# Low weight parts made during the feed-forward and fetched later from DRAM; a branch's input split in halves

## Chip, core and metric

The kernel runs on one core of a Trainium2 chip. It is one program with one instruction stream for each engine: TensorE (PE in the profile; its weight loads are PEld), VectorE (DVE), ScalarE (ACT), GpSimd (POOL) and SyncE (SP), whose stream here only issues DMAs. The metric is the device time in microseconds (us) of one execution, the median of several runs.

## What is computed

Two transformer blocks in a row on 512 tokens of width 1024. The first is a recurrent mixer, a gated feed-forward and a small gate. The second has two attentions and a feed-forward with 16384 experts. What the change touches, from the reference:

```python
def hybrid_layer(...):            # first block
    ...                           # mixer; x = x + merged @ w_out
    h = rmsnorm(x, g_ffn)
    g, u = jnp.split(h @ w_gate_up, 2, axis=-1)
    x = x + (jax.nn.silu(g) * u) @ w_down          # the feed-forward
    gate = jax.nn.sigmoid(rmsnorm(x, g_ple) @ w_ple_gate)
    x = x + gate * (p_i @ w_ple)

def compress(t, w1, w2):          # second block, keys (kv = 0) and values (kv = 1)
    blk = t[:, cmp_idx] + cmp_pos[:, None, :]
    blk = blk.transpose(0, 1, 3, 2, 4).reshape(B, n_cmp, G, CMP_LEN * dk)
    return jax.nn.gelu(blk @ w1) @ w2

def peer_ffn(x, w_q, sub_keys, expert_u, expert_v):
    q = _rms((xt @ w_q).reshape(T, P_HEADS, P_KEY_DIM)).astype(x.dtype)   # queries
    s1 = jnp.einsum('thd,hnd->thn', q[..., :half], sub_keys[:, 0])
    s2 = jnp.einsum('thd,hnd->thn', q[..., half:], sub_keys[:, 1])
    v1, i1 = lax.top_k(s1, P_TOPK)
    v2, i2 = lax.top_k(s2, P_TOPK)
    ...                           # 16 experts e and weights g for each token and head
    a = jnp.einsum('cd,ckd->ck', xc, expert_u[ec])
    w = (gc * jax.nn.gelu(a)).astype(x.dtype)
    return jnp.einsum('ck,ckd->cd', w, expert_v[ec])
```

## The kernel before

**Products.** A float32 product is made of three products of a narrower type (F32R). Each operand is split into a high part (ACT casts it, L58) and a low part (the operand less its high part, on DVE or POOL, L59). `mm3` (L71 to L73) then adds high x high, high x low of the activations and low x high of the weights in PSUM. Weights come in tiles of 128 x 1024. `weights` loads one over SP into `wraw` (three buffers) and splits it into `whi` and `wlo` (two buffers each). `linear` does that and runs 24 matmuls of 512 columns on it.

**Stages**, in the times of the profiled execution. The mixer of the first block lasts to about 369 us. The feed-forward runs from there to some 750 us: 44 `linear`s on `w_gu`, then 8 sums over three pieces of `w_down`. `ple` follows with 8 `linear`s on `w_ple_gate`. The second block's attentions begin near 800 us with the two compressed branches. Its output product ends near 1134 us. The queries of the expert part run to about 1354 us, a table of one-hot products (`build`) to 1532 us, and the dense product over all experts to the end.

**Compressed branches** (`compress`, keys first, then values). From the projection a tile `blk` is made, 128 x 16 x 64. ACT and DVE (for the values POOL) split it into `bs`, of which there is one buffer. Four tiles of `w1` follow, each with 8 matmuls (L949, L950).

**Queries** (`queries`). For each of 8 heads two tiles of `peer_w_q` are multiplied. The low part of the first is made on DVE, of the second on POOL. Between the heads DVE picks the 16 best keys of each half (`choose_steps`), and once, beside heads 0 and 1, it scales the input by its norm (`normalise`: xn, then xsh on ACT and xsl on DVE). All products from head 2 on need that scaled input. Beside the heads run the first chunks of the dense expert part. `hidden` takes one chunk of 128 experts of U (`peer_ut`), multiplies it (24 matmuls of 384 columns into psA) and applies the gelu. The first 16 calls make the chunks of `AWAY` (35, 41, ..., 125), whose results are spilled to DRAM; then come chunks 0, 1, 2 and so on. Nine calls stand between the heads and eleven behind them.

**Order.** The program is written with the Tile language. Its scheduler lays the instructions of each engine into one fixed order, by a simulated time, and each engine then runs its list strictly in that order. A DMA of SP that waits for a buffer holds up all of SP's later DMAs.

## Time and profile before

| | us |
|---|---|
| median of 3 runs (2426.09 to 2430.34) | 2426.5 |
| the profiled execution, its own time | 2424.03 |
| span of its instructions | 2422.3 |
| PE busy, of that span | 2365.4 |
| feed-forward, 369 to 631 us: PE busy | 262.0 of 262 |
| compressed branches, 840 to 865 us: PE busy | 18.0 of 25 |
| queries, 1134 to 1354 us: PE busy | 200.5 of 220 |

PE is busy in 98% of the span, so the table is read for where it is not. Two places stand out: the compressed branches and the first 70 us of the queries. A row of a timeline gives start and duration, engine, line, operation, output and inputs, and in brackets the idle time before it and whose result ended that. A row of the waits gives the total, how often, and the longest. In a row by stages every engine has its busy time, and PEclk is the clock granted to PE as a share of full speed.

### The profile page before, as it was taken

Reading aid. Unit: us, or ns where it says so; the run is one execution under the profiler, and the core shown is the slowest. Engines: PE = TensorE matmul, PEld = TensorE weight load, DVE = VectorE, ACT = ScalarE, POOL = GpSimd, SP = SyncE. Lnnn points to the kernel's source line nnn. Section 1 sums busy time; section 2 is a strip of 40 time slices with the busy share of each in tenths; the row PEclk is TensorE's granted clock in tenths of the full one; section 3 lists DMA queues with packets and bytes.
Section 4 is the critical chain, followed back from the end, with each engine's and each line's share of the span. In section 5 each row is a group of like instructions: output and inputs, shape, how many; then the busy total and the mean of one; then the engine's idle time right before and its main releaser. Section 6 shows DMA issues by size and latency. Waiting matters only on the chain.

```text
span 2422.3 us, 34482 instructions
## 1 busy us (share of the span) xinstructions
PE 2365.4 (98%) x12831; PEld 2027.7 (84%) x12831; DVE 1779.3 (73%) x3426; ACT 1018.3 (42%) x1634; POOL 688.1 (28%) x693
## 2 busy tenths in 40 slices
PE   8999999999999999999799999999899999999999
PEld 7888888888888777677688999998798889989887
DVE  7777664555435658776899898796788878889797
ACT  5444343222224466763344555433333333333333
POOL 1000001000011204334455000255555555555441
PEclk9999999999999999999899999999999999999999
DMA  4232322222333331002133555648999999999895
GB/s 134 96 105 90 102 96 96 96 96 96 97 96 108 106 105 44 1 1 84 59 119 128 179 218 207 226 160 290 333 332 348 350 341 326 351 347 360 302 342 203
DMA packets 166072, 434.37 MB, mean 179 GB/s; under 512 B 15120, under 2 KB 71312, under 8 KB 164368
## 3 DMA queue, kind: packets, MB, share of 16 engines
q1 hardware_dynamic: 126736, 294.80, 36.1%
q0 software_dynamic: 36864, 134.23, 14.8%
q10 hardware_dynamic: 2304, 3.15, 0.3%
q8 instruction: 100, 1.64, 0.3%
q14 instruction: 68, 0.56, 0.1%
HBM read 401.71 MB, written 30.41 MB: 178 GB/s over the span
## 4 chain that ended last, share of the span: by engine, by line
PE 44%; DVE 5%; DMA 2%; ACT 1%; issue 1%; POOL 0%; ACTq 0%; DVEq 0%; POOLq 0%
PE ps L1792 7%; PE ps L1793 7%; PE psA L73 7%; PE psA L71 7%; PE ps L1791 7%; PE psA L72 6%; PE ps L1733 3%; DMA wraw<-peer_ut 1%; DVE wlo L59 1%; DMA wraw<-peer_v 1%; PE ps L73 0%; PE ps L71 0%; DVE ix L1583 0%; PE ps L72 0%; DVE ix L1580 0%
## 5 line engine op out<-in xcount | busy, mean ns | idle before, releaser
L58 ACT CAST whi<-wraw 128x1024 fp32r<-128x1024 f32 (+3 forms) x322 | 330.3, 1026 | 708.9 <-issue 250.1
L59 DVE TENSOR_TENSOR wlo<-wraw,whi 128x1024 fp32r<-128x1024 f32 (+2 forms) x314 | 387.6, 1235 | 205.4 <-ACT whi L58 197.3
L71 PE MATMUL psA<-xsh,whi 128*128 128x384 f32 x1024 | 346.6, 339 | 3.6 <-ACT whi L58 3.3
L73 PE MATMUL psA<-xsh,wlo 128*128 128x384 f32 x1024 | 345.3, 337 | 4.0 <-DVE wlo L59 4.0
L72 PE MATMUL psA<-xsl,whi 128*128 128x384 f32 x1024 | 343.5, 335 | 0.0
L72 PE MATMUL ps<-xl,whi 128*128 128x512 f32 x864 | 337.3, 390 | 4.3 <-DVE xl L64 4.3
L73 PE MATMUL ps<-xh,wlo 128*128 128x512 f32 x864 | 337.8, 391 | 0.5 <-DVE wlo L59 0.5
L71 PE MATMUL ps<-xh,whi 128*128 128x512 f32 x864 | 336.8, 391 | 0.7 <-ACT whi L58 0.5
L1792 PE MATMUL ps<-vl,wh 128*128 128x512 f32 x768 | 299.9, 390 | 3.9 <-DVE vl L59 3.9
L1793 PE MATMUL ps<-vh,wl 128*128 128x512 f32 x768 | 298.1, 389 | 0.0
L1791 PE MATMUL ps<-vh,wh 128*128 128x512 f32 x768 | 243.8, 390 | 4.5 <-ACT vh L58 4.5
L304 POOL TENSOR_TENSOR sq<-sq,sqt 128x512 f32<-128x512 f32 x18 | 28.8, 1601 | 711.9 <-ACT sqt L303 708.3
L71 PEld LDWEIGHTS psA<-xsh,whi 128*128 128x128 f32 x1024 | 192.4, 188 | 10.6 <-ACT whi L58 4.5
L73 PEld LDWEIGHTS psA<-xsh,wlo 128*128 128x128 f32 x1024 | 192.2, 188 | 8.2 <-DVE wlo L59 5.6
L72 PEld LDWEIGHTS ps<-xl,whi 128*128 128x128 f32 x864 | 162.5, 188 | 39.5 <-DVE xl L64 5.5
L72 PEld LDWEIGHTS psA<-xsl,whi 128*128 128x128 f32 x1024 | 192.4, 188 | 2.9
L73 PEld LDWEIGHTS ps<-xh,wlo 128*128 128x128 f32 x864 | 162.4, 188 | 36.9 <-DVE wlo L59 3.2
L71 PEld LDWEIGHTS ps<-xh,whi 128*128 128x128 f32 x864 | 162.5, 188 | 35.2 <-ACT whi L58 1.0
L58 ACT CAST wh<-w 128x384 fp32r<-128x384 f32 x128 | 65.7, 513 | 255.0 <-issue 150.5
L1792 PEld LDWEIGHTS ps<-vl,wh 128*128 128x128 f32 x768 | 144.1, 188 | 32.2 <-DVE vl L59 5.2
L1791 PEld LDWEIGHTS ps<-vh,wh 128*128 128x128 f32 x768 | 143.7, 188 | 32.0 <-ACT vh L58 5.7
L1793 PEld LDWEIGHTS ps<-vh,wl 128*128 128x128 f32 x768 | 144.2, 188 | 28.3
(549 smaller groups left out, 4676.9 us busy)
## 6 DMA issues: line engine op xcount, KB each, us to landing
wraw<-peer_ut SPq DMA_DIRECT2D x128, 512.0 KB, 5.2
wraw<-peer_v SPq DMA_DIRECT2D x128, 512.0 KB, 6.2
wraw<-w_in SPq DMA_DIRECT2D x58, 512.0 KB, 3.3
gdram<-blk SPq DMA_DIRECT2D x12, 2048.0 KB, 7.2
wraw<-w_gu SPq DMA_DIRECT2D x44, 512.0 KB, 3.2
gt<-gdram SPq DMA_DIRECT2D x32, 704.0 KB, 8.1
wraw<-w_out SPq DMA_DIRECT2D x16, 512.0 KB, 3.3
wraw<-peer_w_q SPq DMA_DIRECT2D x16, 512.0 KB, 3.3
```

Source lines behind the costliest of these rows:

```text
L58: s.nc.scalar.copy(hi, raw)
L59: (eng or s.nc.vector).tensor_tensor(lo, raw, hi.bitcast(F32), op=ALU.subtract)
L71: mm(ps, wh, ah[:, ka, :], start=start, stop=False)
L72: mm(ps, wh, al[:, ka, :], start=False, stop=False)
L73: mm(ps, wl, ah[:, ka, :], start=False, stop=stop)
L304: nc.gpsimd.tensor_tensor(sq[:, 0, :], sq[:, 0, :], t, op=ALU.add)
L1733: last = mm(ps[:, i * 128:i * 128 + 128], os[:, j * 4 + i], f[:, j * 4 + i], start=f is f0, stop=f is f2)
L1791: mm(Y[tt][b], wh[:, sl], vh[:, vs], start=False, stop=False, skip_group_check=True)
L1792: mm(Y[tt][b], wh[:, sl], vl[:, vs], start=False, stop=False, skip_group_check=True)
L1793: mm(Y[tt][b], wl[:, sl], vh[:, vs], start=False, stop=last, skip_group_check=True)
```

## The change

- `ahead` is a generator that is stepped during the feed-forward and `ple`. A step takes a quarter tile (128 x 256) of one of the weights that come much later: SP loads it into `alo` (three buffers), ACT casts it into `ahi` (one buffer), DVE subtracts in place, and a DMA issued by POOL writes the low part to the DRAM tile `lows`. `tick` steps it 1.6 times for each `linear`, and in proportion for the pieces of `w_down`.
- `weights` has a new argument `low`. Where it is given, ACT still casts the high part, but the low part comes by a DMA of SP from DRAM into `wlo`. DVE and POOL do nothing.
- The list is the 16 tiles of `peer_w_q` and 20 U chunks (16 of `AWAY`, then 0 to 3). Where the low part lies ready, `hidden_chunk` also puts its 24 matmuls in another order: 8 high x high, 8 high x low, then 8 with the weights' low part.
- `compress` splits `blk` in two halves, in two buffers, both branches on ACT and DVE.

The ticks are 44 x 1.6 + 8 x 22/8 x 1.6 + 8 x 1.6 = 118.4. So 118 of 36 x 4 = 144 steps are made: 29 whole tiles, which are 16 of the queries and 13 of U (35 to 107). The other 7 chunks (113, 119, 125, 0 to 3) take the old way, and two steps are made for nothing.

```diff
+SHARE = 1.6
+EARLY = 36
...
-    def weights(s, src, n, eng=None):
+    def weights(s, src, n, eng=None, low=None):
         raw = s.load(src, n)
...
-        s.split(raw[:, :n], hi[:, :n], lo[:, :n], eng)
+        if low is None:
+            s.split(raw[:, :n], hi[:, :n], lo[:, :n], eng)
+        else:
+            s.nc.scalar.copy(hi[:, :n], raw[:, :n])
+            s.nc.sync.dma_start(lo[:, :n].bitcast(F32), low)
         return hi, lo
+
+    def ahead(s, todo):
+
+        nc = s.nc
+        d = s.dram.tile([len(todo), 128, D], F32, name="lows")
+        for i, (key, src) in enumerate(todo):
+            for q in range(4):
+                sl = slice(q * 256, q * 256 + 256)
+                lo = s.home.tile([128, 256], F32R, tag="alo", name=s.name("alo"), bufs=3)
+                hi = s.home.tile([128, 256], F32R, tag="ahi", name=s.name("ahi"), bufs=1)
+                nc.sync.dma_start(lo.bitcast(F32), src[:, sl])
+                s.split(lo.bitcast(F32), hi, lo)
+                nc.gpsimd.dma_start(d[i][:, sl], lo.bitcast(F32))
+                if q == 3:
+                    s.low[key] = d[i]
+                yield
+
+    def tick(s, share):
+        if s.early is not None:
+            s.due += share
+            while s.due >= 1:
+                s.due -= 1
+                next(s.early, None)
...
@@ linear
+        s.tick(SHARE)
         return ps
@@ ffn
+            s.home, s.early = fa, s.ahead(s.later())
...
+                    s.tick(SHARE * (k1 - k0) / 8)
@@ ple
+            s.home = la
...
+            s.early = None
@@ compress
-        bs = ap.tile([128, 16, 2, 64], F32R, tag="bs", name=s.name("bs"))
-        s.split(blk, bs[:, :, 0, :], bs[:, :, 1, :], s.nc.gpsimd if kv else None)
+        bs = [ap.tile([128, 8, 2, 64], F32R, tag="bs", name=s.name("bs"), bufs=2) for _ in range(2)]
+        for hf in range(2):
+            s.split(blk[:, hf * 8:hf * 8 + 8], bs[hf][:, :, 0, :], bs[hf][:, :, 1, :])
...
+    def later(s):
+
+        u = list(AWAY) + list(range(LAG))
+        todo = [(("q", i), s.I["peer_w_q"][i]) for i in range(16)] + [(("u", c), s.I["peer_ut"][c]) for c in u]
+        return todo[:EARLY]
@@ queries
-            w = [s.weights(I["peer_w_q"][2 * h + half], D, G if half else V) for half in range(2)]
+            w = [s.weights(I["peer_w_q"][2 * h + half], D, G if half else V, s.low.get(("q", 2 * h + half))) for half in range(2)]
@@ hidden_chunk
+        low = s.low.get(("u", c))
+        w = s.weights(s.I["peer_ut"][c], D, eng, low)
...
+            for i, j in ((0, 0), (0, 1), (1, 0)):
+                for k in range(KD):
+                    s.nc.tensor.matmul(ps[:, :TD], w[i][:, k * 128:k * 128 + 128], x[j][:, k, :], start=i + j + k == 0, stop=i == 1 and k == KD - 1)
```

**What SP issues in the feed-forward.** Before, at its beginning (`wraw` is a weight tile's buffer, `w_gu` the gate and up weights):

```order
L47 DMA wraw_2992<-w_gu 128x1024
L47 DMA wraw_3023<-w_gu 128x1024
L47 DMA wraw_3063<-w_gu 128x1024
L47 DMA wraw_3094<-w_gu 128x1024
L47 DMA wraw_3134<-w_gu 128x1024
```

After, at the same place:

```order
L53 DMA wraw_3102<-w_gu 128x1024
L76 DMA alo_3044<-peer_w_q 128x256
L76 DMA alo_3081<-peer_w_q 128x256
L76 DMA alo_3087<-peer_w_q 128x256
L53 DMA wraw_3145<-w_gu 128x1024
L76 DMA alo_3133<-peer_w_q 128x256
L76 DMA alo_3139<-peer_w_q 128x256
L53 DMA wraw_3191<-w_gu 128x1024
```

Two or three quarter loads have moved between each two weight loads: 104 of the 118 stand between the fourth load of `w_gu` and the 43rd, that is within 39 weight loads, and none stands beside `w_down`. The other 14 stand in `ple`. From the fourth on, each of them waits for the POOL DMA that empties the buffer of the third before it.

**What ACT does in the compressed branches.** Before (`whi` is a tile of `w1`, `bs` the branch's input, `low` the end of the first branch's product):

```order
L58 CAST whi_6019<-wraw_6017 128x1024
L58 CAST whi_6033<-wraw_6031 128x1024
L58 CAST whi_6056<-wraw_6054 128x1024
L785 COPY rcq<-ps_6130 128x4
L786 ACTIVATE rcq<-ps_6130 128x4
L58 CAST whi_6070<-wraw_6068 128x1024
L952 COPY low_6045<-ps_5988 64x256
L58 CAST bs_6050<-blk_5863 128x16x64
```

After:

```order
L91 CAST whi_6747<-wraw_6745 128x1024
L91 CAST bs_6764<-blk_6574 128x8x64
L91 CAST whi_6773<-wraw_6771 128x1024
L823 COPY rcq<-ps_6847 128x4
L824 ACTIVATE rcq<-ps_6847 128x4
L91 CAST whi_6787<-wraw_6785 128x1024
L992 COPY low_6759<-ps_6702 64x256
L91 CAST bs_6765<-blk_6574 128x8x64
```

The first half of the values' `bs` has moved ahead of the end of the keys' product; the second half stands where the whole stood.

**What SP issues at the start of the queries.** Before (`keys` are the sub-keys of a head):

```order
L47 DMA wraw_9232<-peer_w_q 128x1024
L47 DMA wraw_9238<-peer_w_q 128x1024
L47 DMA wraw_9316<-peer_w_q 128x1024
L47 DMA wraw_9322<-peer_w_q 128x1024
L1429 DMA keys_9359<-keys 128x256
L1429 DMA keys_9529<-keys 128x256
L47 DMA wraw_9637<-peer_w_q 128x1024
```

After (`wlo` is the buffer of a tile's low part):

```order
L53 DMA wraw_9949<-peer_w_q 128x1024
L53 DMA wraw_9955<-peer_w_q 128x1024
L53 DMA wraw_10033<-peer_w_q 128x1024
L64 DMA wlo_9952<-lows 128x1024
L53 DMA wraw_10039<-peer_w_q 128x1024
L64 DMA wlo_9958<-lows 128x1024
L53 DMA wraw_10354<-peer_w_q 128x1024
L1475 DMA keys_10076<-keys 128x256
L1475 DMA keys_10246<-keys 128x256
L64 DMA wlo_10036<-lows 128x1024
```

Each tile now has two DMAs, and that of the low part stands one or two tiles behind that of the whole.

## Rows read from the trace of the kernel before

**Rows 1.** The page, part 1: engine, busy us (share), instructions.

```profile
PE 2365.4 (98%) x12831; PEld 2027.7 (84%) x12831; DVE 1779.3 (73%) x3426; ACT 1018.3 (42%) x1634; POOL 688.1 (28%) x693
```

**Rows 2.** Busy by stage: us, PE, PEld, DVE, ACT, POOL, PEclk, DMA share, GB/s.

```profile
369.00:631.00 262.00, 262.00 (x1170) 215.90 (x1169) 135.72 (x167) 80.77 (x104) 7.13 (x4) 1.00 0.30 96
840.00:865.00 25.00, 17.98 (x97) 15.20 (x96) 14.65 (x17) 12.84 (x18) 3.65 (x2) 0.80 0.50 147
1134.00:1180.00 46.00, 35.70 (x173) 27.57 (x173) 31.92 (x121) 19.05 (x37) 17.25 (x27) 0.89 0.25 80
1180.00:1207.00 27.00, 22.18 (x98) 18.04 (x97) 22.53 (x102) 8.67 (x15) 14.45 (x21) 0.87 0.18 64
1207.00:1354.00 147.00, 142.63 (x783) 129.96 (x782) 131.51 (x581) 67.51 (x121) 65.88 (x117) 1.00 0.38 122
```

**Rows 3.** Waits of PE: line, waited for, us in total, times, longest.

```profile
PE ps L71 <- ACT xsh L63: 8.4, 2, 6.1
PE ps L949 <- POOL bs L59: 4.9, 1, 4.9
PE ps L73 <- DVE wlo L59: 4.8, 2, 4.3
...
PE psA L73 <- DVE wlo L59: 4.0, 5, 1.6
```

**Rows 4.** Timelines of the compressed branches: PE, then POOL.

```profile
856.87 0.58 PE L949 MATMUL ps<-whi,bs 128*128 128x256 f32 x1 [4.90 <-POOL bs L59]
...
854.48 2.34 POOL L59 TENSOR_TENSOR bs<-blk,bs 128x1024 fp32r<-128x1024 f32 x1 [9.85 <-ACT bs L58]
```

**Rows 5.** Timelines of the queries: DVE, then POOL.

```profile
1134.22 0.69 DVE L664 TENSOR_TENSOR x<-wo,wo 128x512 f32<-128x512 f32 x1 [1.18 <-POOL wo L663]
...
1138.92 2.83 DVE L664 TENSOR_TENSOR x<-wo,wo 128x512 f32<-128x512 f32 x1 [1.86 <-POOL wo L663]
...
1164.35 2.50 DVE L64 SCALAR_TENSOR_TENSOR xsl<-xn,c_vec,xsh 128x384 fp32r<-128x384 f32 x1
...
1169.49 0.59 DVE L64 SCALAR_TENSOR_TENSOR xsl<-xn,c_vec,xsh 128x384 fp32r<-128x384 f32 x1
...
1189.12 2.44 DVE L1623 CAST pf<-pos 128x48 f32<-128x48 uint32 x2
...
1138.84 2.36 POOL L59 TENSOR_TENSOR wlo<-wraw,whi 128x1024 fp32r<-128x1024 f32 x1
...
1164.07 2.36 POOL L59 TENSOR_TENSOR wlo<-wraw,whi 128x1024 fp32r<-128x1024 f32 x1 [10.15 <-ACT whi L58]
...
1189.17 2.34 POOL L59 TENSOR_TENSOR wlo<-wraw,whi 128x1024 fp32r<-128x1024 f32 x1 [6.54 <-ACT whi L58]
```

**Rows 6.** Timelines of the feed-forward: SP, then DVE, then ACT.

```profile
442.60 16.65 SPq L47 DMA_DIRECT2D wraw<-w_gu  x4
...
441.34 1.22 DVE L59 TENSOR_TENSOR wlo<-wraw,whi 128x1024 fp32r<-128x1024 f32 x1 [0.21 <-ACT whi L58]
...
456.58 1.05 ACT L58 CAST whi<-wraw 128x1024 fp32r<-128x1024 f32 x1 [3.85 <-issue]
```

**Rows 7.** The page, part 6, DMAs: count, KB each, median us from issue to landing.

```profile
wraw<-w_gu SPq DMA_DIRECT2D x44, 512.0 KB, 3.2
...
spill<-gl ACTq DMA_DIRECT2D x16, 192.0 KB, 2.6
...
wraw<-w_ple SPq DMA_DIRECT2D x8, 128.0 KB, 2.0
```

**Rows 8.** Instructions on tiles lwh, lwl and peer_u: ns min/median/max; landing of peer_u's DMAs.

```profile
L58 ACT CAST lwh<-wraw x8: 392/402/407, 751.2 to 795.6; 128x256 fp32r<-128x256 f32 x8
L59 DVE TENSOR_TENSOR lwl<-wraw,lwh x8: 411/416/2022, 752.5 to 798.3; 128x256 fp32r<-128x256 f32 x8
...
L1847 POOL DMA_INDIRECT x<-peer_u,ei x74: 932/1677/1989, 1657.6 to 1996.1; - x74
...
DMA to landing us min/median/max: 4.9/8.1/11.8
```

More of the change, by code (lines that the diff above doesn't have):

```diff
@@ L31, in __init__ @@
         s.wp = ctx.enter_context(tc.tile_pool(name="wp", bufs=2))
+        s.dram = ctx.enter_context(tc.tile_pool(name="dr", bufs=1, space=bass.MemoryType.DRAM))
         s.psum_stack = ctx.enter_context(ExitStack())
         s.n = 0
+        s.low = {}
+        s.early = None
+        s.due = 0.0
         s.banks(8)
@@ L279, in ple @@
                 made = []
+            s.early = None
         return x1
@@ L948, in compress @@
                 j = q * 4 + i
-                mm(ph[:, 0:256], bs[:, j].rearrange("p a b -> p (a b)"), wh[:, i, :], start=j == 0, stop=False, skip_group_check=True)
-                mm(ph[:64, 0:256], bs[:, j, 0, :], wl[:, i, :], start=False, stop=j == 15, skip_group_check=True)
+                mm(ph[:, 0:256], bs[j // 8][:, j % 8].rearrange("p a b -> p (a b)"), wh[:, i, :], start=j == 0, stop=False, skip_group_check=True)
+                mm(ph[:64, 0:256], bs[j // 8][:, j % 8, 0, :], wl[:, i, :], start=False, stop=j == 15, skip_group_check=True)
         low = ap.tile([128, 256], F32, tag="low", name=s.name("low"), bufs=1)
@@ L1671, in hidden_chunk @@
     def hidden_chunk(s, c, eng):
-        w = s.weights(s.I["peer_ut"][c], D, eng)
+        low = s.low.get(("u", c))
+        w = s.weights(s.I["peer_ut"][c], D, eng, low)
         ps = s.pp.tile([128, 512], F32, tag="po", name=s.name("psA"), bufs=2)
-        for k in range(KD):
-            s.mm3(ps[:, :TD], w, (s.xh[:, :, 128:], s.xl[:, :, 128:]), k, k, k == 0, k == KD - 1)
+        x = s.xh[:, :, 128:], s.xl[:, :, 128:]
+        if low is None:
+            for k in range(KD):
+                s.mm3(ps[:, :TD], w, x, k, k, k == 0, k == KD - 1)
+        else:
+            for i, j in ((0, 0), (0, 1), (1, 0)):
+                for k in range(KD):
+                    s.nc.tensor.matmul(ps[:, :TD], w[i][:, k * 128:k * 128 + 128], x[j][:, k, :], start=i + j + k == 0, stop=i == 1 and k == KD - 1)
         g = s.ring.tile([128, TD], F32, tag="gl", name=s.name("gl"))
```

## Prediction

> **What bounds the kernel now.** I read the page's busy times first: PE is busy 2365.4 of 2422.3 us [rows 1]. So nothing but PE's idle time and its low clock can be won, some 57 us of the one and a little of the other. The table by stages says where they lie [rows 2]. In the feed-forward PE is busy in all 262 us; a gain there is impossible, a loss is not. In the compressed branches it is busy 18.0 of 25 us, in the first 73 us of the queries 57.9 us, at a granted clock of 0.80 and of 0.87 to 0.89. In the 147 us behind that, 4.4 us are idle. The list of PE's waits then names who ends them [rows 3]: POOL's `bs` 4.9 us in the branches; in the queries xsh (ACT) 8.4, `wlo` (DVE) 4.8 in two waits and 4.0 in five small ones. DVE, the engine that the change relieves there, is not itself the bound: 131.5 of 147 us busy while PE has 142.6.
>
> **The change, part by part.**
>
> *Compressed branches.* Before, the values' `bs` could only be made when the keys' product had released the one buffer. ACT cast it, POOL took 2.34 us for the low part, and PE stood 4.90 us [rows 4]. Now the first half is cast and subtracted while the keys' second half is still multiplied, so this wait goes. What is late next is the split of the `w1` tiles: ACT 1.05 us and then DVE 1.2 us for every tile, with two buffers, and the second half of `bs` and a table load stand between them on ACT. I take a gain of 4 us, bounds 2 (half of the wait comes back at the third tile) and 6 (the wait and the low clock: 0.2 of 25 us is 5 us at most, of which I count one).
>
> *Queries, what is removed.* 8 low parts of 128 x 1024 on POOL and 8 on DVE for the queries, 13 on DVE for U. On DVE that is 21 x 1.2 = 25 us, nearly all beside a busy PE and worth nothing. What counts is where PE waits. (a) At 1138.92 the last residual sum on DVE took 2.83 us, against 0.69 for the same one before it, while POOL ran a split from 1138.84 on, for 2.36 us [rows 5]. PE waits for its xsh (2.3 of the 8.4 us). Without POOL's split: -2.1. (b) At 1164.35 the same with `xsl` of the normalisation, 2.50 us against 0.59, beside POOL's split at 1164.07 [rows 5]. It stands in the chain that ends PE's 6.1 us [rows 3]: -1.9. The chain itself, DVE's choice of keys mixed with eight xn and xsl, stays and is late next. (c) PE's 4.3 us for `wlo`: DVE's cast of pos took 2.44 us beside POOL's split at 1189.17 [rows 5], and `wlo` came behind it. Now a DMA brings that low part; it lands 3.2 us after its issue, going by a weight load of that size [rows 7], which is about when the ACT cast and the sub-key products are through. I take -3, and -1 for the clock that stays up (27 us at 0.87 lost 3.5 us in all). (d) The small waits for `wlo` under psA, 4.0 us: -2.5, since 13 of the 20 chunks no longer need DVE, and their low part is only read at the seventeenth of 24 matmuls. Sum -10.5.
>
> *Queries, what is added.* 29 DMAs of 512 KB behind the others in SP's list. Each waits until PE has released `wlo` two tiles before, and behind it wait the loads of the next tiles and of the sub-keys. From the release it has the whole tile between as cover, 24 matmuls or 5.4 us (see below), against 3.2 us to land, or 4.9 us, the quickest landing of a 512 KB gather in the busy last stage [rows 8]. So it is hidden on both prices, by 0.5 to 2.2 us; I take +0.5 in all, bounds 0 and +8. Queries together: -10, bounds -15 and -2.
>
> *Feed-forward, what is added.* 118 steps: on ACT 118 x 0.40 = 47 us, on DVE 118 x 0.42 = 50 us [rows 8]. DVE then has 135.7 + 44 = 180 of 262 us and ACT 80.8 + 42 = 123 (104 steps) [rows 2]: room in sum. The DMAs, 256 KB a step, double the 96 GB/s and the 0.30 share. The danger is the order. 104 steps stand among 39 weight loads in SP's list. One `linear` takes (16.65 - 0.33)/3 = 5.44 us (four issues, the last one 0.33 long) [rows 6], so PE needs 39 x 5.44 = 212 us for them. A quarter load may only go when its buffer's last content has reached DRAM; with three buffers 104 steps take 104/3 = 34.7 times the round trip c of one buffer. Behind a late quarter load waits the next weight load. Such a load is now issued early: that of 442.60 lands 3.2 us later, at 445.8, and is cast at 456.58, 10.8 us later [rows 6, 7]; the cast runs some 3.2 us ahead of need (5.44 less 1.05 and 1.2). So PE begins to stand at 34.7 c > 212 + 14, that is from c = 6.5 us.
>
> What is c? The load of 128 KB lands in 2.0 us [rows 7]. Cast and subtraction: 0.40 and 0.42 [rows 8]. Two hand-overs of 0.2, as DVE waits for ACT's cast [rows 6]. The store by a DMA of POOL is not in the trace. The nearest row is the spill, 192 KB on ACT's queue, 2.6 us [rows 7]; by the slope between 128 and 512 KB (1.2 us on 384 KB) 128 KB would take 2.4. POOL's issue is longer than SP's: 0.93 at the least against 0.33 [rows 6, 8], so +0.6: 3.0 us. From below 2.0, as a load; from above 4.9, the gather. So c = 2.0 + 0.82 + 0.4 + 3.0 = 6.2, between 5.2 and 8.1, not counting turns on ACT and DVE. At 6.2 the steps take 215 us and are covered, with 0.3 us a step to spare. I take 0, bounds 0 and 34.7 x 8.1 - 226 = +55.
>
> The Trainium skill prices this store lower. Its page "DMA: Bandwidth & Descriptors", section "Anatomy of one DMA — SWDGE (gpsimd) path", gives such a DMA a fixed 2.0 us and its bytes at 436 GB/s, an estimate of 2.3 us for 128 KB. By it c would be 5.5 and the steps 191 us, covered with ease. The trace's only DMAs of POOL do not agree with so low a fixed part: 4.9 us at the least, for 512 KB [rows 8]. The same section warns that the receipt of a write to DRAM can be long, which no run here shows yet.
>
> *The 14 steps in `ple`*: 14 x 0.42 us on DVE beside a PE that has no listed wait there. Nothing, bounds 0 and +3.
>
> **Sum.** -4 - 10 + 0 = -14 us on the profiled execution's 2424.0, so 2410.0. That execution stood 2.5 us under the median, 2426.5; on the median's scale it is 2412.5.
>
> **The rivals.** (A) is the above. Its own range is 2405 to 2422, by the bounds of the branches and the queries.
>
> (B) SP's list is throttled by the three buffers: the wait on POOL's store takes the place of DVE's and POOL's work, in the stage where PE had no idle time at all. Against it: c = 6.2 by the nearest rows. For it: the margin is 0.3 us a step, turns on ACT (123 of 262 us) and DVE (180) and the single `ahi` come on top, and the list is so dense (2.7 quarter loads to a weight load) that nothing but c sets its speed. It decides from c = 6.5 and costs 34.7 us for each us above. At 6.9 the gain is gone (-14 + 13); at 7.3, which I take for its size, the time is 2412.5 + 28 = 2440; at 8.1, 2468. The skill has a rule that would feed it: "SBUF — State Buffer", section "Who interferes with whom", says that DVE in certain modes keeps GpSimd from writing the descriptors of its DMAs. POOL's issue here ranges from 0.93 to 1.99 us beside a busy DVE, which bears out a delay of 1 us at most; that would give c = 7.2.
>
> (C) The fetched low parts are late in the queries: in SP's list they stand behind loads that wait themselves, and a query tile reads its low part at the third matmul. At 0.35 us for each of 29, +10: -4 - 10 + 10 gives 2422.5, no change. For it: PE's release, not time, starts each fetch, so a second of two tiles that end together is late. Against it: the cover of 5.4 us.
>
> (D) The change does less than it says: 29 of 36 tiles are made, and the waits (a) and (b) return because DVE's choice of keys fills the room. Then -4 - 4 = 2418.5.
>
> **How the numbers follow.** A 0.50, B 0.30, C 0.12, D 0.08. About 0.2%, 4.9 us, is what a measurement of this kernel can tell from no change, so faster means below 2421.6, slower above 2431.4. Faster: A but for 0.02, 0.05 of C (some fetches in time) and 0.05 of D: 0.58. Slower: 0.24 of B. The same: 0.02 of A, 0.06 of B (c from 6.8 to 7.0), 0.07 of C, 0.03 of D: 0.18. The predicted time is A's. The range reaches from 2402, a little below A's best, to 2446, which leaves out the upper third of B (0.10) and little else.
>
> **What would show it.** In the profile after, the feed-forward should have PE busy without a gap and `linear`s 5.44 us apart. If B holds, PE's waits there name `whi` or `wlo`, SP's weight loads stand more than 5.44 us apart, and SP's waits name DMA `lows`. The landing time of `lows<-alo` on the page settles c: up to 3.3 us for A, more for B. In the branches the wait on `bs` should be gone. In the queries (a) shows as a sum of 0.7 us on DVE, (b) as no `xsl` over 1 us, (c) and (d) as no wait of PE for a `wlo` from DVE beyond the seven old chunks. If C holds, PE waits there for DMA `wlo<-lows`. The prediction is wrong at its root if the feed-forward is unchanged and the queries win nothing: then PE's waits there hung on the chain of the choice of keys and not on the splits.

## The result: slower by 0.6%, with the gain there and a larger loss in front of it

The changed kernel takes 2440.7 us in the median of nine runs, the kernel before 2426.5; the ratio is 1.0061 (95% interval 1.0045 to 1.0076). The profiled execution has a span of 2434.8 us against 2422.3. So +14 us where -14 was forecast: the size and the place of rival (B), 2440 us in the feed-forward, not of (A). (The two profiled executions are 12.5 us apart; that is what the stages below add up to.)

Page, part 1, of the changed kernel, the line that answers to [rows 1]:

```profile
PE 2373.9 (97%) x12831; PEld 2020.5 (83%) x12831; DVE 1791.5 (74%) x3526; ACT 1065.0 (44%) x1754; POOL 722.2 (30%) x802
```

PE has the same 12831 matmuls and more idle time. Where it lies is read from the table by stages, with the columns of [rows 2]. Its stretches begin and end where the work of before's stretches now lies: w_gu's linears, w_down, the per-layer gate (before 733 to 800), the compressed branches, the queries' first 73 us and the 147 behind them:

```profile
369.00:656.35 287.35, 273.40 (x1170) 212.36 (x1169) 171.34 (x272) 121.84 (x209) 64.28 (x109) 1.00 0.58 184
656.35:758.35 102.00, 102.00 (x452) 84.46 (x451) 33.13 (x35) 28.32 (x34) 7.75 (x5) 1.00 0.32 95
758.35:831.30 72.95, 69.75 (x320) 55.95 (x319) 48.89 (x61) 37.88 (x63) 23.12 (x20) 1.00 0.46 149
871.30:891.70 20.40, 16.15 (x97) 12.92 (x96) 15.76 (x20) 12.22 (x19) 1.32 (x1) 0.92 0.62 179
1157.60:1227.70 70.10, 63.90 (x312) 51.22 (x311) 49.70 (x242) 30.23 (x55) 26.18 (x44) 0.98 0.48 159
1227.70:1365.60 137.90, 136.13 (x754) 125.01 (x753) 106.78 (x542) 66.02 (x117) 48.16 (x112) 1.00 0.59 198
```

Before, the gate's stage was this (the other rows of before are in [rows 2]):

```profile
733.00:800.00 67.00, 67.00 (x312) 54.79 (x311) 41.23 (x48) 34.01 (x50) 16.91 (x7) 1.00 0.35 112
```

The first row after holds the same 1170 matmuls as before's 262 us in 287.35. The change is best followed by one instruction that both kernels have: how much later it starts than before. Such landmarks are DVE's `wlo` at 373 us, PE's last matmul of `w_down` (750.09 before, 775.44 after), DVE's `vcb` (809.07, 840.37), `krs` (881.57, 908.26) and `rb` (1141.89, 1165.53), and POOL's first `gt` (1535.33, 1546.95). The differences between neighbours are the price of each stage, in us. The last two columns are experiments told below:

| stage, between two landmarks | forecast | changed kernel | paced, 29 tiles | paced, 33 tiles, five buffers |
|---|---|---|---|---|
| feed-forward (373 to the gate's stage) | 0 (0 to +55) | +25.4 | +0.2 | 0.0 |
| per-layer gate (to 809) | 0 (0 to +3) | +6.0 | 0.0 | 0.0 |
| compressed branches (to 882) | -4 (-6 to -2) | -4.6 | -3.1 | -3.6 |
| output projection (to 1142) | -2.1 | -3.1 | -3.1 | -3.3 |
| queries (to 1535) | -7.9 | -12.0 | -13.7 | -13.2 |
| rest, to the end | 0 | +0.9 | +2.2 | -1.0 |

The forecast's gain is there and larger, 19.7 us where 14 were counted. It is outweighed by 31 us in two stages that were taken to cost nothing. (The first 20 us of the program, until PE has its first weights, differ by up to 3.4 us between profiled executions of any kernel here; the landmarks begin behind them.)

### Where the 25 us come from

Waits of SP's queue in the changed kernel, 369 to 820 us (for which transfer, us, times, longest):

```profile
SPq L76 <- DMA lows<-alo: 195.5, 84, 5.7
SPq L53 <- DVE wlo L92: 159.2, 40, 5.9
```

SP stands 84 times in front of a quarter load because the buffer's last content has not reached DRAM. Before, it only stood for raw weight buffers. And PE, which waited for nothing in that stretch, now does (369 to 760):

```profile
PE ps L106 <- DVE wlo L92: 10.6, 24, 0.5
PE ps L104 <- ACT whi L91: 3.2, 6, 0.8
```

Timelines of that kernel, SP, ACT, DVE, POOL and PE, put together; the first five lines are one buffer's round, the other five the weight load behind it:

```profile
442.14 1.96 SPq L76 DMA_DIRECT2D alo<-peer_w_q  x3
444.72 0.41 ACT L91 CAST ahi<-alo 128x256 fp32r<-128x256 f32 x1 [2.15 <-DMA alo<-peer_w_q]
445.15 0.43 DVE L92 TENSOR_TENSOR alo<-alo,ahi 128x256 fp32r<-128x256 f32 x1 [1.51 <-ACT ahi L91]
445.88 0.54 POOL L78 DMA_DIRECT2D lows<-alo  x1 [3.73 <-DVE alo L92]
448.86 0.98 SPq L76 DMA_DIRECT2D alo<-peer_w_q  x2
...
444.19 0.38 SPq L53 DMA_DIRECT2D wraw<-w_gu  x1
447.61 1.04 ACT L91 CAST whi<-wraw 128x1024 fp32r<-128x1024 f32 x1
448.69 1.22 DVE L92 TENSOR_TENSOR wlo<-wraw,whi 128x1024 fp32r<-128x1024 f32 x1
448.70 0.50 PE L104 MATMUL ps<-xh,whi 128*128 128x512 f32 x1 [0.32 <-ACT whi L91]
449.96 0.50 PE L106 MATMUL ps<-xh,wlo 128*128 128x512 f32 x1 [0.52 <-DVE wlo L92]
```

A round is 442.14 to 448.86, 6.7 us. The weight load of 444.19 goes out behind its quarter loads, is cast 3.4 us later, and PE begins with it 1.1 us after that: there is no time in hand any more, where before a cast stood 10.8 us behind the landing of its load [rows 6, 7]. A stall listed as 0.5 us costs 0.7, since the list counts only what lies beyond the modelled end of the matmul ahead: matmuls that start 0.23 us apart stand 0.93 apart there. Thirty stalls make 18.7 us so, and the matmuls just before and behind a stall, which start 0.1 us late, 6.2 more: 25.0 in all, where the same sum over before's starts is 0.7.

### The profile page after: what moved, and what is told of

Read it like the earlier page. It is cut to its first block, busy times and chain, and to the rows that moved or that the text cites. A ratio compares the mean times of both kernels' runs of the same rounds, so it can differ in the third digit from the quotient of the medians.

```text
span 2434.8 us, 35457 instructions
## 1 busy us (share of the span) xinstructions
PE 2373.9 (97%) x12831; PEld 2020.5 (83%) x12831; DVE 1791.5 (74%) x3526; ACT 1065.0 (44%) x1754; POOL 722.2 (30%) x802
## 4 chain that ended last, share of the span: by engine, by line
PE 72%; DVE 9%; issue 8%; DMA 6%; ACT 2%; POOL 2%; SPq 0%; POOLq 0%; ACTq 0%; DVEq 0%
PE ps L106 9%; PE ps L104 8%; PE ps L105 8%; PE ps L1846 6%; PE ps L1847 6%; PE ps L1845 6%; PE psA L106 6%; PE psA L104 6%; PE psA L105 6%; PE ps L1787 3%; PE ps L615 2%; POOL lows L78 2%; DMA wraw<-peer_ut 2%; DVE wlo L92 1%; PE ps L1297 1%
## 5 line engine op out<-in xcount | busy, mean ns | idle before, releaser
L91 ACT CAST whi<-wraw 128x1024 fp32r<-128x1024 f32 (+2 forms) x293 | 299.6, 1023 | 465.8 <-PE ps L105 189.7
L92 DVE TENSOR_TENSOR wlo<-wraw,whi 128x1024 fp32r<-128x1024 f32 (+2 forms) x293 | 359.6, 1228 | 171.4 <-ACT whi L91 162.6
L104 PE MATMUL psA<-xsh,whi 128*128 128x384 f32 x920 | 311.4, 338 | 2.6 <-ACT whi L91 2.6
L106 PE MATMUL psA<-xsh,wlo 128*128 128x384 f32 x920 | 309.9, 337 | 1.2 <-DVE wlo L92 1.1
L105 PE MATMUL psA<-xsl,whi 128*128 128x384 f32 x920 | 308.5, 335 | 0.0
L1845 PE MATMUL ps<-vh,wh 128*128 128x512 f32 x768 | 250.8, 390 | 3.3 <-ACT vh L91 3.0
L104 PEld LDWEIGHTS psA<-xsh,whi 128*128 128x128 f32 x920 | 172.8, 188 | 8.3 <-ACT whi L91 3.8
L106 PEld LDWEIGHTS psA<-xsh,wlo 128*128 128x128 f32 x920 | 172.7, 188 | 4.5 <-DVE wlo L92 2.7
L105 PEld LDWEIGHTS psA<-xsl,whi 128*128 128x128 f32 x920 | 172.9, 188 | 2.6
L92 DVE TENSOR_TENSOR vl<-wraw,vh 128x1024 fp32r<-128x1024 f32 x128 | 156.1, 1220 | 20.4 <-ACT vh L91 18.3
```

The costliest lines, as they stand in the source:

```text
L91: s.nc.scalar.copy(hi, raw)
L92: (eng or s.nc.vector).tensor_tensor(lo, raw, hi.bitcast(F32), op=ALU.subtract)
L104: mm(ps, wh, ah[:, ka, :], start=start, stop=False)
L105: mm(ps, wh, al[:, ka, :], start=False, stop=False)
L106: mm(ps, wl, ah[:, ka, :], start=False, stop=stop)
L1845: mm(Y[tt][b], wh[:, sl], vh[:, vs], start=False, stop=False, skip_group_check=True)
```

## The experiments

The theory, T: SP's list goes at the pace of its quarter loads, and three buffers with a round trip of 7 us are too few for 2.67 of them to a weight load. The main rival, W: the steps' work is too much for ACT, DVE or the DMA rings beside a busy PE.

### Pacing the quarter loads

The same work, but a quarter load may not stand in SP's list ahead of its own linear's weight load:

```diff
-        s.nc.sync.dma_start(t[:, :n], src)
+        s.wload = s.nc.sync.dma_start(t[:, :n], src).ins
...
-                nc.sync.dma_start(lo.bitcast(F32), src[:, sl])
+                with s.tc.issue_after(s.wload):
+                    nc.sync.dma_start(lo.bitcast(F32), src[:, sl])
```

> The changed kernel with one thing more: a quarter load may not go into SP's list ahead of the weight load of its own linear, so that about 1.6 quarter loads stand between two weight loads of the feed-forward instead of 2.67, and the rest of the 118 lie under w_down and the per-layer gate. The same work, spread thinner. Theory T (the loss is SP's list: three buffers, a round trip c of 7.0 us as traced, so 2.67 x 7.0 / 3 = 6.2 us for a weight load against 5.44 that PE needs): 1.6 x 7.0 / 3 = 3.7 us, covered; the 25 us of the feed-forward go, all but 1 or 2 at its first linears, where the list is as dense as before; the 6 us of the gate stage stay. About 2440.7 - 24 = 2416.5 us. Rival W (the work itself is too much for DVE, ACT or the DMA rings beside a busy PE): the same 118 steps still cost over 15 us in the feed-forward and w_down, 2430 to 2440 us.

Measured: 2412.5 us, ratio to the kernel before 0.9944 (0.9924 to 0.9963), 4 us under what was expected. PE lists no wait at all between 369 and 700 us, and SP's waits for the stores are fewer (369 to 760):

```profile
SPq L77 <- DMA lows<-alo: 50.5, 21, 5.1
```

By the landmarks the feed-forward costs 0.0 us, the gate's stage +7.4. W falls: beside a busy PE the 105 steps of the feed-forward are free if they are spread. The second paced kernel also takes the steps out of the gate's stage:

```diff
-SHARE = 1.6
-EARLY = 36
+SHARE = 1.8
+EARLY = 29
```

> As the paced kernel, with 29 tiles asked for and 1.8 steps to a linear, so that the same 29 tiles are done by the end of w_down and no step stands in the per-layer gate's stage. T: 1.8 x 7.0 / 3 = 4.2 us for a load in the linears, covered; nothing in w_down (1.7 x 7.0 / 3 = 3.9 of 4.99 us). If the gate stage's 6 us come from the steps (their two-input DVE subtractions and stores put between POOL's sums), they go as well: 2410 to 2411 us. If these 6 us come from something else in that stage (the place of POOL's sums, the phase in which the stage is entered), they stay: 2416 us. W: 2430 to 2440 us.

Measured: 2405.0 us, ratio 0.9911 (0.9888 to 0.9933), 21 us under the kernel before, 36 under the changed one and 5 under what was expected. Table by stages of this kernel, the feed-forward and the gate:

```profile
369.60:631.60 262.00, 262.00 (x1169) 215.67 (x1168) 165.67 (x250) 112.84 (x188) 52.70 (x88) 1.00 0.56 180
733.80:800.80 67.00, 67.00 (x312) 54.82 (x311) 41.29 (x48) 34.00 (x50) 16.91 (x7) 1.00 0.35 112
```

PE is busy throughout, with DMA at 0.56 and 180 GB/s beside it. So the 6 us of the gate's stage came from the steps in it. (By SP's list in the trace they are 13, with 105 among w_gu's loads; ahead of the prediction they were counted as 14 and 104.) PE has three listed waits there, 4.1 us together. How the two longest came about, the changed kernel's timelines show (DVE, POOL, PE):

```profile
801.62 5.03 DVE L97 SCALAR_TENSOR_TENSOR yl<-x,gfn,yh 128x512 fp32r<-128x512 f32 x1 [1.15 <-ACT yh L96]
806.57 1.21 DVE L92 TENSOR_TENSOR wlo<-wraw,whi 128x1024 fp32r<-128x1024 f32 x1
...
819.66 1.82 DVE L92 TENSOR_TENSOR alo<-alo,ahi 128x256 fp32r<-128x256 f32 x1 [1.06 <-ACT ahi L91]
...
801.32 2.42 POOL L92 TENSOR_TENSOR w<-wraw,w 128x1024 fp32r<-128x1024 f32 x1
803.68 2.41 POOL L661 TENSOR_TENSOR sq<-sq,sq2t 128x1024 f32<-128x1024 f32 x1
...
807.84 0.50 PE L106 MATMUL ps<-xh,wlo 128*128 128x512 f32 x1 [1.80 <-DVE wlo L92]
...
822.66 0.50 PE L106 MATMUL ps<-xh,wlo 128*128 128x512 f32 x1 [1.30 <-DVE wlo L92]
```

`yl`, 0.75 us elsewhere, lasts until POOL's two operations are over, and `wlo` behind it is late. POOL's pair is there before too, but beside DVE work that PE did not need next; the steps shifted the order so that it fell on `yl`. The second wait stands behind a step's own subtraction at 819.66, 1.82 us instead of 0.43 beside a sum on POOL. That these shifts are the whole cause is inferred; that the steps are is shown.

### The making and the halves by themselves

The kernel before with the halves alone (the diff of `compress`, nothing else), and the changed kernel with the low parts made and none fetched:

```diff
-                    s.low[key] = d[i]
+                    pass
```

> The kernel before with the second part of the change alone: the compressed branches' input parts in two halves. From the changed kernel's trace, where that stage is 4.6 us shorter: 2426.5 - 4.6 = 2422 us, PE's wait of 4.9 us for bs gone. Rival: the gain in that stage came from the shifted phase of the stage before it (PE entered it 31 us later with other loads in flight), and the halves alone give 0 to 2 us: 2425 to 2426.5.

Measured: 2421.2 us, ratio 0.9980 (0.9967 to 0.9993). PE's wait for `bs` is gone; what is late next is `wlo`, as forecast (840 to 870 us, before 1.7 us in three waits):

```profile
PE ps L952 <- DVE wlo L59: 3.7, 4, 1.2
```

> The changed kernel with the making of the low parts as it is and none of them fetched: the queries work as in the kernel before. What it measures is the price of the making alone. T: 25 us in the feed-forward and 6 us in the gate stage stand, the 4.6 us of the halves are won, the 15 us of the queries are not: 2426.5 + 31 - 4.6 = 2453 us, with 84 waits or so of SP for the stores. Rival: part of the 31 us belongs to the fetching (its loads queue behind others) or part of the queries' gain to the delayed phase: under 2447 us.

Measured: 2457.2 us, ratio 1.0124 (1.0101 to 1.0147). By the landmarks the feed-forward and the gate's stage cost 32.5 us, the branches win 3.0, the stage up to 1142 costs 2.1, and the queries cost 3.0 instead of winning 12; where these 3 come from is open. (Of the 2.1, 1.9 arise in the attentions, where the clock granted to PE from 990 to 1005 us is 0.66 against 0.77 before, from 960 to 975.) SP stands 84 times for the stores as in the changed kernel, 194.8 us in all. So the loss belongs to the making, and the queries' gain comes only when the low parts are fetched.

### How many buffers: two and five

> The changed kernel with two buffers alo instead of three. Its SP list has 2 quarter loads to a weight load where it had 2.67, over more loads: 80 steps among w_gu's loads, 23 under w_down. Theory T (the list goes at the pace of steps per load x c / buffers): with fewer loads in flight c is a little shorter, 6.3 us (the least of the parts in the changed kernel's trace is 5.6, the mean 7.0), so 2 x 6.3 / 2 = 6.3 us a load against 5.44: +0.86 x 40, and against 4.99 in w_down +1.3 x 12: +50 in place of +25, about 2440.7 + 25 = 2465 us (2445 to 2480). Rival: what counts is how many quarter loads stand between two weight loads (2 instead of 2.67), or the total of the work: then the loss shrinks or stays, 2430 to 2441 us.

The edit is `bufs=3` to `bufs=2` at `alo`. Measured: 2450.9 us, ratio 1.0105 (1.0089 to 1.0122). The direction is T's, against the rival by which fewer quarter loads to a weight load lose less. By PE's first matmul of `w_down`, w_gu's linears lose 26.1 us, 0.64 a load where 0.86 were expected; under w_down it is 12.2 where 15 were expected, so T overstates in both places. SP's waits (369 to 800):

```profile
SPq L76 <- DMA lows<-alo: 259.0, 102, 5.6
```

> The changed kernel with five buffers alo; the tile ft of the feed-forward has one buffer instead of two, to make room. The list now has 4 quarter loads to a weight load, over 26 weight loads, then none. T: 4 x c / 5; with c 7.0 it is 5.6 us a load, +0.2 x 26 = +4; but the four go out together and pass the one ahi and DVE one by one, so that c may grow to 8: 6.4, +25. I expect c = 7.5, +15, and so 2440.7 - 10 = 2430 us (2415 to 2441). Rival S (more buffers are more slack): the feed-forward loses nothing, 2415 us, with SP's waits for the stores gone.

The edit is `bufs=5`, and `bufs=1` for `ft`. Measured: 2436.8 us, ratio 1.0055 (1.0039 to 1.007); the feed-forward loses 26.4 us, near the 25 that T gives for c = 8. S falls: the list is planned as dense as the buffers permit (four quarter loads to a weight load), so more buffers alone bring no slack.

```profile
SPq L76 <- DMA lows<-alo: 121.9, 61, 5.5
```

The round trip, from one load of a buffer to the next load of it, averaged over the 105 steps of the feed-forward (for two and five buffers likewise):

| part, us | forecast | three buffers (least) | two | five |
|---|---|---|---|---|
| SP's load to ACT's cast | 2.0 | 3.00 (2.30) | 2.70 | 3.57 |
| cast to DVE's subtraction | 0.6 | 0.50 (0.43) | 0.46 | 0.48 |
| subtraction to POOL's issue | 0.6 | 0.72 (0.66) | 0.72 | 0.72 |
| POOL's issue to the next load | 3.0 | 2.77 (2.06) | 2.37 | 3.71 |
| sum c | 6.2 | 6.97 | 6.25 | 8.50 |

The more quarters go out together, the longer each takes. The store itself was priced high enough, not too low. What grew is the load. ACT waits before a cast of `ahi` mostly for the landing of the load, and little for DVE to release the one `ahi` (changed kernel, 389 to 656 us):

```profile
ACT ahi L91 <- DMA alo<-peer_w_q: 71.6, 51, 3.6
ACT ahi L91 <- DMA alo<-peer_ut: 49.1, 31, 3.8
ACT ahi L91 <- DVE alo L92: 9.8, 18, 1.0
```

The trace also holds the completion marks of each DMA. By them a quarter load lands 2.83 us after its issue on average (2.23 at the least): 2.45 us when no other quarter load is under way, 2.87 beside one, 3.72 beside two. The cast follows 0.16 us after the landing.

### What the queries' gain is made of

The kernel before with POOL's eight subtractions for the queries put on DVE:

```diff
-            w = [s.weights(I["peer_w_q"][2 * h + half], D, G if half else V) for half in range(2)]
+            w = [s.weights(I["peer_w_q"][2 * h + half], D, V) for half in range(2)]
```

> The kernel before, with the queries' eight subtractions that POOL makes put on DVE; nothing is made ahead or fetched. It separates two reasons for the queries' gain of 15 us. Theory P (POOL's subtraction lengthens the DVE operation beside it): the last sum and the xsl go back from 2.8 and 2.5 us to 0.7 and 0.6, PE's waits there shrink as in the changed kernel, by 3.1 at the sum and 4.0 at the xsl; against it DVE makes eight subtractions more, 9.6 us, and comes later at some wlo (0 to 5 us). 2426.5 - 7 + 3 = 2422 us (2418 to 2426). Theory Q (the gain comes from DVE having less to do): with more on DVE the queries grow, 2427 to 2435 us.

Measured: 2424.3 us, ratio 0.9999 (0.9989 to 1.0009): no change in the whole, and both theories are right in their place. From 1100 to 1215 us, the output projection's end and the first part of the queries, it is 9.6 us faster; from there to 1535 us it gives back 8.1. (The branches, which the edit leaves alone, were 2.5 us shorter in this execution, with a granted clock of 0.95 from 820 to 890 us where it was 0.90 before; by the end 1.4 us were left.) PE's waits (1126 to 1370 us):

```profile
PE psA L73 <- DVE wlo L59: 6.7, 4, 3.0
PE ps L73 <- DVE wlo L59: 4.5, 3, 2.6
PE ps L71 <- ACT xsh L63: 2.0, 1, 2.0
```

The 8.4 us for xsh [rows 3] are 2.0, and in the program nothing has changed but POOL's place: POOL's subtraction held up the DVE operations beside it. (The scheduler lays DVE's list anew for every kernel, and part of the 2.0 may come of that: the third and fourth `xn` start 1.1 us apart here and 3.6 before.) The last residual sum, 2.83 us at 1138.92 before [rows 5], is at 1138.09 in this kernel (and at 1164.69 in the changed one):

```profile
1138.09 0.69 DVE L664 TENSOR_TENSOR x<-wo,wo 128x512 f32<-128x512 f32 x1 [1.18 <-POOL wo L663]
```

The wait for `wlo` under the chunks grew from 4.0 to 6.7 us, as theory Q says of a DVE with eight subtractions more. The next two kernels are paced and take one half of the list each, the 16 query tiles or the 13 U chunks:

```diff
-SHARE = 1.6
-EARLY = 36
+SHARE = 1.0
+EARLY = 16
```

> The paced kernel with the 16 query tiles alone (64 steps, 1.0 to a linear, none in the gate's stage) and no U chunk. What it lacks against the paced kernel with 29 tiles (2405 us) is the 13 U chunks. By the traces the waits for wlo under the chunks shrink from 4.0 us to 0.4 with them, and the reordered matmuls have some part: 3 to 4 us, so 2408 to 2409 us. Rival: the U chunks are worth nothing, since the queries' gain frees DVE anyway: 2405 us; or more than half of the gain: over 2413 us.

Measured: 2419.5 us, ratio 0.9981 (0.9968 to 0.9994), 10 us above what was expected. PE's waits (1126 to 1370 us), and the timelines of the longest one (ACT, DVE, PE):

```profile
PE psA L107 <- DVE wlo L93: 10.3, 3, 5.9
PE ps L105 <- ACT xsh L97: 2.1, 1, 2.1
...
1205.60 1.05 ACT L92 CAST whi<-wraw 128x1024 fp32r<-128x1024 f32 x1 [0.24 <-PE ps L106]
...
1208.50 0.48 DVE L1629 MAX8 v<-sc 128x8 f32<-128x128 f32 x2
1208.90 1.85 DVE L1674 TENSOR_TENSOR oh<-iota,pf 128x480 f32<-128x480 f32 x3
1212.36 1.48 DVE L93 TENSOR_TENSOR wlo<-wraw,whi 128x1024 fp32r<-128x1024 f32 x1
...
1213.89 0.69 PE L107 MATMUL psA<-xsh,wlo 128*128 128x384 f32 x1 [5.90 <-DVE wlo L93]
```

The U chunk's cast ends at 1206.65; its `wlo` comes on DVE at 1212.36, behind the choice of keys that stands ahead of it in DVE's list. PE reaches the chunk earlier, since the first part is faster, and waits there.

```diff
-        todo = [(("q", i), s.I["peer_w_q"][i]) for i in range(16)] + [(("u", c), s.I["peer_ut"][c]) for c in u]
+        todo = [(("u", c), s.I["peer_ut"][c]) for c in u]
```

> The paced kernel with the 13 U chunks alone made ahead (52 steps, none in the gate's stage) and the 16 query tiles split as before, half on POOL and half on DVE. With the kernel that has the halves alone (2421), the one with the query tiles alone (2419.5) and the one with both (2405) it fills a square of four. Theory I (the two parts work only together: POOL's splits hold up the first 73 us, and what the first part then wins is lost again at the next U chunk whose low part stands behind DVE's choice of keys): U alone leaves the 6.1 us wait for xsh and the 4.3 us wait for wlo where they were and wins at most its own 4 us of small waits: 2417 us (2415 to 2420). Rival: the parts add up, and U alone carries the difference between the two measured ones: 2421 - 14 = 2407 us.

Measured: 2420.1 us, ratio 0.9980 (0.9968 to 0.9991). PE's waits of the same stretch:

```profile
PE ps L105 <- ACT xsh L97: 8.4, 2, 6.1
PE ps L107 <- DVE wlo L93: 6.7, 3, 4.3
...
PE psA L107 <- DVE wlo L93: 0.9, 1, 0.9
```

So the square of four, as ratios to the kernel before: halves alone 0.9980, with the query tiles 0.9981, with the U chunks 0.9980, with both 0.9911. Neither part is worth anything that can be measured; together they are worth 0.7%, 17 us. With the query tiles alone the first part's gain is lost at the next chunk, with the chunks alone the first part's waits stay. Two things are not told apart here: the fetch of a chunk's low part and the new order of its 24 matmuls, which always come together.

### How dense the list may be

> The paced kernel with 33 tiles instead of 29, 2.0 steps to a linear (17 U chunks instead of 13). T: 2.0 x 7 / 3 = 4.7 us a load, still under 5.44, and in w_down 1.8 x 7 / 3 = 4.3 of 4.99: the feed-forward costs 0 to 2 us. Four chunks fewer for DVE in the queries, where with 29 tiles PE has only one wait of 0.4 us for a wlo from DVE left: worth 0 to 2 us. 2404 us (2402 to 2407). Rival: the list is already too dense: 2410 us or more.

Measured: 2416.8 us, ratio 0.9957 (0.994 to 0.9974). A miss: the feed-forward costs 9.2 us. In the queries the four chunks more bring nothing (-16.3 us from the output projection's last products on, -16.8 with 29 tiles).

```profile
SPq L77 <- DMA lows<-alo: 210.6, 65, 6.5
```

> The paced kernel with all 36 tiles, 2.2 steps to a linear: the nearest to the edge that still has no step in the gate's stage. T: 2.2 x 7 / 3 = 5.1 us a load on average against 5.44 and 2.0 x 7 / 3 = 4.7 against 4.99, but loads with three steps (7 us) come up to twice in a row, more often at the start: 2 to 6 us lost, against 0 to 2 won: 2408 us (2404 to 2413). If it costs 20 us and more, what counts is the sum of the steps and not their pace: 2425 us.

Measured: 2430.1 us, ratio 1.0017 (1.0001 to 1.0032); the feed-forward costs 25.8 us. A miss too, nearer to the number that was to speak against T. Both expectations carried the 7.0 us of the dense list over to a looser one. Measured in the same way, c is 8.0 and 7.7 us here, but it is 8.6 with 29 tiles, where nothing is lost. This c runs to the next load of the buffer, so it contains SP's own turn, and steps times c over buffers is little more than the time that SP's list took. What tells the kernels apart is the round from a quarter load's issue to the landing of its store, by the completion marks in the trace. For w_gu's linears alone, in us, where PE needs 5.44 for a load:

| kernel | steps to weight loads | c to the next load | round to the landing | steps a load x round / buffers | lost |
|---|---|---|---|---|---|
| changed, three buffers | 105 to 39 | 6.97 | 6.88 | 6.17 | 25.4 |
| two buffers | 82 to 41 | 6.26 | 6.21 | 6.21 | 26.1 |
| five buffers | 105 to 27 | 8.50 | 8.29 | 6.45 | 26.4 |
| paced, 29 tiles | 79 to 41 | 8.61 | 8.12 | 5.22 | 0.2 |
| paced, 33 tiles | 88 to 41 | 8.01 | 7.75 | 5.54 | 7.2 |
| paced, 36 tiles | 96 to 41 | 7.66 | 7.50 | 5.86 | 16.9 |
| paced, 33 tiles, five buffers | 88 to 41 | 12.80 | 9.52 | 4.09 | 0.0 |

The linears lose where the product is over 5.44 and nowhere else, and the excess times the loads gives each loss to within some 5 us. (What is left of the 9.2 and 25.8 is lost under w_down.) That a round is longer in the looser lists goes with when the quarter loads go out: 44 of 76 with 29 tiles, and 25 of 102 in the changed kernel, are issued while a weight load is under way. Those land after 3.9 and 3.4 us, the others after 2.4 and 2.7. That it is the buffers and not the sum of the steps was put to a last run, 33 tiles with five buffers:

```diff
-                lo = s.home.tile([128, 256], F32R, tag="alo", name=s.name("alo"), bufs=3)
+                lo = s.home.tile([128, 256], F32R, tag="alo", name=s.name("alo"), bufs=5)
...
-                g, t = (fk.tile([128, T], F32, tag=n, name=s.name(n)) for n in ("fg", "ft"))
+                g, t = (fk.tile([128, T], F32, tag=n, name=s.name(n), bufs=b) for n, b in (("fg", 2), ("ft", 1)))
```

> The paced kernel with 33 tiles, as before with three buffers alo (2417 us, 9 us lost in the feed-forward, where 1.8 steps to a linear lost none), now with five buffers and one buffer ft. Theory B (what is short is buffers in flight: at 2.15 quarter loads to a weight load the round trip was 8.05 us, 2.15 x 8.05 / 3 = 5.8 us a load): with five it is 3.5 us, the 9 us go: 2417 - 9 = 2408 us (2405 to 2411). It tells too whether the one buffer ft costs anything by itself, since then a loss stays. Rival O (the places in ACT's and DVE's lists: a cast ahi stands in front of the cast of the next weight tile and holds it up until its quarter has landed, however many buffers there are): the loss stays, 2414 to 2420 us.

Measured: 2405.6 us, ratio 0.9911 (0.9892 to 0.993), 11 us under the same kernel with three buffers; the feed-forward costs 0.0. SP's waits for the stores are all but gone (369 to 760):

```profile
SPq L77 <- DMA lows<-alo: 11.8, 6, 5.5
```

O falls, the one buffer `ft` costs nothing, and T holds in this form: pace and buffers together decide. Five buffers with an unpaced list lose 26 us, three with 2.1 steps to a load lose 9, five with 2.1 none. This kernel and the paced one with 29 tiles are equal, and both beat the two kernels of the study.

## Why the prediction was wrong, point by point

**What bounds the kernel.** Right: only PE's idle time could be won, and a loss in the feed-forward was possible. Wrong was that DVE "is not itself the bound" in the 147 us: its sum left room, but PE waits there for single operations that stand behind long runs of others in DVE's list, as the 5.9 us of the run with the query tiles alone show.

**Compressed branches.** -4, measured -4.6 in the changed kernel and -3.0 to -5.6 in the other kernels with halves; `wlo` is late next, as said. The granted clock rose from 0.80 to 0.92, which the forecast counted at 1 us.

**Queries, removed.** (a) -2.1, measured -3.1 at DVE's `rb` and -2.2 at PE's own next matmuls; PE's wait is gone. (b) -1.9, measured -4: the wait of 6.1 us for xsh is 2.0 in the changed kernel. One `xsl` alone was lengthened, and that is the 1.9; the other 2 us go with the new order of DVE's list, in which the third and fourth `xn` stand closer, and their cause is not shown. (c) -3 and (d) -2.5: the 4.3 us for DVE's `wlo` are gone, with 2.5 us of waits for fetched low parts in their place, and the 4.0 us became 0.4. ([rows 3] counts the whole program: in the queries it was 4.3 in one wait, not 4.8 in two, and 3.9 in four, not 4.0 in five.) PE's waits of the changed kernel in the queries (1157 to 1366 us):

```profile
PE ps L106 <- DMA wlo<-lows: 2.5, 3, 1.2
PE ps L105 <- DVE xsl L97: 2.3, 2, 1.5
PE ps L104 <- ACT xsh L96: 2.0, 1, 2.0
PE ps L104 <- ACT whi L63: 0.7, 2, 0.5
PE psA L106 <- DVE wlo L92: 0.4, 1, 0.4
```

So -10.5 measured -15.1. Some of it may be the clock: 0.98 was granted in the first 70 us against 0.87 to 0.89 before [rows 2], where the forecast counted 1 us; no run separates it. The terms were added as if each stood by itself; the square of four shows that they don't.

**Queries, added.** +0.5 for the fetches: PE waits 2.5 us for them in three places, well within the bounds. (C) did not come.

**Feed-forward: the step that failed.** The formula was right, the value of c was not: 6.2 forecast, 6.97 measured, with the threshold at 6.5. The term that was mis-sized is the first of the sum, the quarter's load. It was taken at 2.0 us, the median landing of a load of that size in another stage [rows 7]; beside the other quarter loads and the weight load it landed after 2.83 us on average. The "turns on ACT and DVE", which the text named and did not price, were not the error: the cast follows the landing by 0.16 us, and from there to POOL's issue it took 1.22 us where 1.2 was forecast. Nor was the store: forecast at 3.0, it took 2.77 with SP's wait for its turn. Beside that, of the 14 us that the weight loads' early issue was to absorb, about 5 were there: 34.7 x 6.97 = 242 us against the 212 + 25 = 237 that the loads took, so most of the excess became PE's loss. With c = 7 in the prediction's own sum the feed-forward costs 17 us and the time is 2429 us, no gain any more; the missing slack makes the rest. The prediction had the margin before it, 0.3 us a round, and gave rival (B) 0.30.

The Trainium skill's page "DMA: Bandwidth & Descriptors", section "Anatomy of one DMA — SWDGE (gpsimd) path", from which 2.3 us was estimated for the store, agrees with the trace: 2.06 us at the least, 2.49 in the median and 2.77 on average from POOL's issue to the next load. The gather, the only kind of DMA of POOL in the trace of before, did not. The c that came of that estimate, 5.5, is farther from 6.97 than the forecast's 6.2, since the load was too short in both.

**The gate's stage.** 0, bounds 0 and +3; measured +6.0. The text counted 14 x 0.42 us on DVE and did not look at POOL's operations of 2.4 us in that stage, though it had read such a one as the cause of the same lengthening in the queries.

**Range and rivals.** 2440.7 lies in the range. (B)'s size of 28 us for c = 7.3 came near 25.4 by luck, since c was 6.97 and most of the 14 us of slack were missing; that the whole came out at its 2440 is luck too, since the gain was 6 us larger and the gate's stage cost 6. (D) was wrong on (a) and (b): they did not return.

## What to carry to other kernels

Where a stream of small steps shares an in-order queue with loads that feed the critical engine, count steps per load times round trip over buffers against the time between loads. Take the round trip from a load's issue to the landing of its store, with every step as it runs in a burst, and a margin of a few per cent as none. A planner fills such a list as far as the buffers allow by its own idea of the round trip: bind each step to the load that it may follow, and then add buffers. Two parts of a change that are each worth nothing alone can be worth something together, as here where the second wait ate what the first gave back; try the parts alone and together.

## What the runs showed of the hardware

A DVE operation with two inputs in SBUF can be held up until the POOL operations beside it end: 5.03 us instead of 0.75 for `yl` over two POOL operations of 2.42 and 2.41 that end at 806.09, with `yl` ending at 806.65. Moving POOL's subtractions away brought the last residual sum from 2.83 to 0.69 us, and PE's wait for xsh from 8.4 to 2.0. The Trainium skill, page "SBUF — State Buffer", section "Who interferes with whom", says that a DVE instruction with two SBUF inputs contends with a GpSimd instruction that reads SBUF; this trace agrees, and it shows that DVE can lose to two in a row. A 128 KB load landed after 2.45 us with no other such load under way and after 3.72 us beside two, in the changed kernel's feed-forward. The DMA rings carried 180 GB/s at a share of 0.56 beside a PE that was busy all of 262 us, at no cost.
